# A hybrid attention and state-space block on one core: products without a reader at the start, projection rows without halos, chunk parts in one PSUM bank, another order of units

## The chip, the cores and the metric

The kernel runs on one NeuronCore of a Trainium2 chip. The metric is the device time of one execution in microseconds (us). Three runs of the kernel before took 896.91, 897.30 and 897.51 us; their median is 897.3 us. Five engines work side by side: TensorE (PE, with its weight loads listed as PEld), VectorE (DVE), ScalarE (ACT), GpSimd (POOL) and SyncE (SP, which here only issues DMAs). Every one of them works through its own list of instructions in order; semaphores tie the lists together.

## What is computed

One encoder layer over 16 meta tokens and 512 tokens (528 rows of 1024 features). One normalised input `u` is projected to all columns that two branches need: an attention branch (MLA) and a bidirectional state-space branch (SSD, chunks of 128 rows, 32 heads in 4 groups). Cut to what matters here:

```python
u = rmsnorm(h, norm_w)                       # h = meta tokens and x, 528 rows
proj = u @ w_in                              # 1024 x 8928: q_lat, kv_lat, k_rope, g_attn, z, xbc, dt_raw, merge
xbc = silu(conv(xbc, conv_w, 5 taps) + conv_b)   # along the rows; 3072 columns = x (2048), B (512), C (512)
dt = softplus(dt_raw + dt_bias)
# per direction and chunk c of 128 rows, per head:
y_diag = (C_c B_c^T * decay) @ (x_c * dt_c)
y_off  = exp(cumsum dA) * (C_c @ state_before_c)
y = y_f + y_b + d_skip * x
y = rmsnorm_per_group(y * silu(z)) @ w_ssd_proj
y_a = (softmax(q k^T) v * silu(g_attn)) @ w_attn_proj
out = rmsnorm(h + (sig(gA) * y_a + sig(gS) * y) @ w_out)[16:]
```

## The kernel before

**Numbers.** Large products are made from float32 split into two parts of the type fp32r, a high one and a low one: `hi*hi + lo*hi + hi*lo`. So a projection of 128 output columns over 1024 features is three runs of 8 matmuls. Plain float32 products and transposes are used in the SSD core.

**Layout of u.** `uh` and `ul` (L464, L465) hold the two parts of u transposed, 8 tiles of 128 features by LP = 536 columns: 4 zero columns, 528 rows, 4 zero columns.

**Start.** Four blocks of x rows and the meta rows are loaded (`LOADS`, L478 on). `nwb` is the norm weight, spread over 128 partitions by two one-row products with `ones` (L490 to L492). Per block `u_stats`, `u_scale` and `u_split` (from L571) make the row scale, the scaled rows `xw`, and by 8 transposes into two PSUM banks `tr` the parts `uh` (a cast on ACT) and `ul` (a subtraction on DVE). Blocks go in the order 3, 2, 1, 0, meta.

**Projections.** `proj` (L532) makes a unit of 128 columns. With the tag "d" it writes a PSUM tile of two banks, one half of the 528 rows in each, the second half of the rows first. `conv_tile` (L741) makes 128 columns of x, B or C. Its `proj_halo` computes 270 columns for each half of the rows (`HALO`): 264 and three on each side, so that the convolution needs no column of the other bank. Then ACT multiplies the middle tap, DVE adds the other four taps with `scalar_tensor_tensor`, and a tanh and a last DVE operation make the silu; each of these works on `[128, 2, 264]`. There are 24 such units, 6 for each of the 4 groups (`in_units`). `silu_tile` makes a unit of z or of the attention gate, 512 columns in one bank of the tag "m". There are two tiles of the tag "d" (PSD) and four banks of the tag "m" (PSM).

**SSD core.** Per group g: `ssd_cb`, `ssd_weight` (8 times; makes the weights M of four heads), `ssd_tok` (transposes of x), `ssd_state`, `ssd_cross` (makes `yo`, the part from the state, in two "d" banks) and `ssd_y` (L948). For each of 4 chunks `ssd_y` transposes `yo` into a bank `yt`, adds it to `x4` on DVE, then multiplies x by M into a second bank `yd` (8 float32 products of 64 output columns, two listed matmuls each) and adds that to `x4` too.

**Order.** The kernel records all operations first. `drive` hands out steps of the main chains and of a queue of fill units; `_Recorder.order` then places every operation in a list of its own making, with a table of assumed durations. Nothing is placed by hand but the order in which units enter the queue: the string `"1a2345bcd"` (L1502) for group 0 (digits are conv units of group 0, letters its four z units) and `"zizizizipipipp"` (L1519) for the groups after: `z` a z unit of this group, `i` a conv unit of the next, `p` an output projection unit of the group before. `i` and `p` both wait for the normalisation of the group before (`epi_ok`).

Weights come through two raw buffers `wr` of 512 KB; ACT casts the high part `wh`, DVE makes the low part `wl`.

Of the kernel before, what the change touches and what calls it, by code (L numbers as in the profile page):

```python
# [22 lines left out]
U0 = 4  # L23
LP = U0 + L + 4
HALO = U0 + HALF + 2
# [243 lines left out]
class _Eng:  # L269
# [3 lines left out]
    def __getattr__(self, op):  # L273
        fn = getattr(self.eng, op)

        def call(*args, **kw):
# [31 lines left out]
            if self.name == "PE":  # L308
                if op == "transpose":
# [49 lines left out]
def hybrid_block_kernel(ctx, tc, a, out):  # L359
# [103 lines left out]

    uh = keep([P, KD, LP], F32R, name="uh")  # L464
    ul = keep([P, KD, LP], F32R, name="ul")  # L465
    for t in (uh, ul):
        V.memset(t[:, :, :U0].bitcast(F32), 0.0)
        V.memset(t[:, :, U0 + L:].bitcast(F32), 0.0)
# [6 lines left out]
    for step in LOADS:  # L475
# [7 lines left out]
        else:  # L483
            c = int(step)
            t = xt[c] = big([P, D], name="xt")
            if c == NC:
                Q.dma_start(t[:NM], a["meta_tokens"])
            else:
                S.dma_start(t, a["x"][0, c * P:(c + 1) * P, :])
    nwb = [psm([P, 512], name="nwb") for _ in range(2)]  # L490
    for j in range(2):
        mm(nwb[j], ones[:1, :], nw[j][:1, :])  # L492

# [38 lines left out]
    def proj(w, src, cols, M=P, tag="m", width=HALF):  # L532
# [7 lines left out]
        for h, s in list(enumerate(parts))[::-1]:  # L540
            o = ps[:M, :cols.stop - cols.start] if tag == "m" else ps[:M, h, :width]
# [5 lines left out]
        return o if tag == "m" else ps[:M, :, :width]  # L547

    def proj_all(w, src, M=P):
        return proj(w, src, U_HALVES if src is u_src else HALVES, M, "d")  # L550

    def proj_halo(w):

        return proj(w, u_src, [slice(0, HALO), slice(HALF, HALF + HALO)], P, "d", HALO)

    def halves(ap):
        return ap.rearrange("p (a b) -> p a b", a=2)

    u_src = [(uh[:, k, :], ul[:, k, :]) for k in range(KD)]
    QRY, HALVES = slice(U0 + NM, U0 + L), (slice(0, HALF), slice(HALF, L))  # L560
    U_HALVES = tuple(slice(U0 + s.start, U0 + s.stop) for s in HALVES)

# [24 lines left out]
    def u_split(c):  # L587
        R = rows(c)
        for j in range(2):
# [3 lines left out]
            uc = slice(U0 + col(c).start, U0 + col(c).stop)  # L593
# [56 lines left out]
    def dt_stage():  # L650
# [7 lines left out]
        A.activation(halves(y[:64]), ps[:64], AF.Identity, bias=dtb[:, 0:1])  # L658
        A.copy(halves(kr[64:96]), ps[64:96])
# [81 lines left out]
    def conv_tile(c0, t, out):  # L741
        w = yield from w_cols(c0)
        o = out()
        ps = yield from proj_halo(w)
        wdone()
        yield has("chv")
        at = lambda d: ps[:, :, U0 + d:U0 + d + HALF]
        A.activation(halves(o), at(0), AF.Identity, bias=cb_(t), scale=cw(2, t))
        yield
        for tap in (0, 1, 3, 4):  # L750
            V.scalar_tensor_tensor(halves(o), at(tap - 2), cw(tap, t), halves(o), op0=ALU.mult, op1=ALU.add)
            if tap == 1:
                yield
        yield
        th = ps[:, :, :HALF]
        A.activation(th, halves(o), AF.Tanh, scale=0.5)
        yield
        V.scalar_tensor_tensor(halves(o), th, 1.0, halves(o), op0=ALU.add, op1=ALU.mult)
# [189 lines left out]
    def ssd_y(g):  # L948
        s = grp[g]
        x4 = s["x"]  # L950
        for c in range(NC):
            yield has(("yo", g, c))
            pyo = yield from bank("m", [P, 4, P], "yt")
            for ti in range(4):
                T.transpose(pyo[:, ti, :], s["yo"][c][:, 2 * ti:2 * ti + 2, :].rearrange("p h d -> p (h d)"), ident)
            yield has(("x", g))
            tt(V, x4[:, :, col(c)], x4[:, :, col(c)], pyo, ALU.add)
            drop("m")
            yield has(("M", g, 2 * c), ("t", g, c))
            pyd = yield from bank("m", [P, 4, P], "yd")  # L960
            for hb_ in range(2):
# [3 lines left out]
                for ti in (2 * hb_, 2 * hb_ + 1):  # L965
                    for e in range(2):
                        hh = 2 * ti + e
                        mm(pyd[64 * e:64 * e + 64, ti, :], s["t"][c][:, hh, :], m[:, hh - 4 * hb_, :])
                done.add(("ydh", g, 2 * c + hb_))
            yield  # L970
# [92 lines left out]
    def kvl_unit(t):  # L1063
# [5 lines left out]
        A.copy(halves(z), ps)  # L1069
# [78 lines left out]
    def k_unit(p):  # L1148
# [6 lines left out]
        for e in range(2):  # L1155
            yield lambda: score_ok(2 * p - 2 + e)
            r = slice(64 * e, 64 * e + 64)
            A.copy(halves(kst[r, 2 * e, :]), ps[r])
            yield
            lo_of(V, halves(kst[r, 2 * e + 1, :]), ps[r], halves(kst[r, 2 * e, :]))  # L1160
# [341 lines left out]
    for k in "1a2345bcd":  # L1502
        fill([first[int(k)] if k.isdigit() else zs["abcd".index(k)]], lambda: True)
    for g in range(NG):
# [14 lines left out]
        for k in "zizizizipipipp":  # L1519
# [79 lines left out]
```

## Time and profile before

| what | us |
|---|---|
| three runs, median | 897.3 |
| the profiled execution, its own time | 898.46 |
| its span, first to last instruction | 896.7 |
| PE busy (98% of the span) | 875.1 |
| DVE busy (79%) | 707.8 |
| ACT busy (61%) | 544.2 |

The profile is of one execution. Between its own time and its span lie 1.8 us, which no instruction of the program fills. An engine counts as busy while one of its instructions is under way. Matmuls overlap in the array: a listed matmul of 128x264 lasts some 0.28 us, while the next one starts 0.12 us after it, so the cost of one in a run is the distance between starts. In a timeline row, `x8` says that eight equal instructions follow each other, and the two numbers ahead are the start of the first and the time from there to the end of the last.

### The profile page before, as it was taken

The numbers are of one execution on the slowest core, as the hardware profiler recorded it, in microseconds if no ns is written. First come the engines' busy times: TensorE is split into PE (matmuls) and PEld (weight loads), VectorE is DVE, ScalarE is ACT, GpSimd is POOL, SyncE is SP. The second block draws the span as 40 slices with busy tenths as digits, with TensorE's granted clock in tenths as the row PEclk, the third lists the DMA queues.
The fourth block names the chain that finished last, engine by engine and source line by source line (L and its number), as shares of the span: only waits on it lengthen the run. The fifth ranks groups of instructions, "written<-read, shape, count | busy, mean of one in ns | idle before, by whom it ended". The sixth has DMA issues, their size and how long they took to land.

```text
span 896.7 us, 13288 instructions
## 1 busy us (share of the span) xinstructions
PE 875.1 (98%) x4984; PEld 723.3 (81%) x4984; DVE 707.8 (79%) x1245; ACT 544.2 (61%) x1159; POOL 13.3 (1%) x20
## 2 busy tenths in 40 slices
PE   7999999999999999999999999999999999999996
PEld 5998779877898778866798888888888888778885
DVE  6798699968996699978859757887788978955464
ACT  6359468955794458866235446777577768643232
POOL 1000000000000000000001000000000000000000
PEclk9999999999999999999999999999999999999999
DMA  7255146432533235542223433132213112154322
GB/s 223 72 144 145 51 122 166 110 95 71 163 121 94 61 105 143 141 116 71 71 88 79 114 79 81 32 75 74 59 45 89 36 45 66 48 199 137 99 83 94
DMA packets 129257, 87.50 MB, mean 98 GB/s; under 512 B 26611, under 2 KB 114328, under 8 KB 129194
## 3 DMA queue, kind: packets, MB, share of 16 engines
q1 hardware_dynamic: 129013, 86.53, 34.6%
q8 instruction: 39, 0.64, 0.3%
q14 instruction: 25, 0.20, 0.1%
q10 hardware_dynamic: 180, 0.14, 0.1%
HBM read 82.32 MB, written 4.33 MB: 97 GB/s over the span
## 4 chain that ended last, share of the span: by engine, by line
PE 84%; DVE 9%; ACT 3%; issue 1%; DMA 1%; POOL 0%; POOLq 0%; SPq 0%; ACTq 0%; DVEq 0%
PE pj L266 58%; PE sc L266 4%; PE wo L266 4%; PE pt L266 3%; PE o L266 3%; PE yo L266 2%; PE st L266 2%; PE yd L266 2%; PE tr L266 2%; PE v L266 2%; DVE wl L266 2%; DVE B L266 1%; DMA ar<-cum_rows 1%; DVE C L266 1%; PE yt L266 1%
## 5 line engine op out<-in xcount | busy, mean ns | idle before, releaser
L266 PE MATMUL pj<-uh,wh 128*128 128x270 f32 (+3 forms) x776 | 161.2, 345 | 5.8 <-DVE x L266 3.1
L266 DVE TENSOR_TENSOR wl<-wr,wh 128x1024 fp32r<-128x1024 f32 (+1 forms) x102 | 123.9, 1217 | 54.0 <-ACT wh L266 53.4
L266 PE MATMUL pj<-uh,wl 128*128 128x270 f32 (+3 forms) x776 | 158.9, 338 | 0.0
L266 PE MATMUL pj<-ul,wh 128*128 128x270 f32 (+3 forms) x776 | 151.5, 336 | 0.0
L266 ACT CAST wh<-wr 128x1024 fp32r<-128x1024 f32 (+1 forms) x102 | 106.2, 1041 | 74.6 <-PE pj L266 54.4
L266 PEld LDWEIGHTS pj<-uh,wh 128*128 128x128 f32 (+1 forms) x776 | 120.9, 190 | 26.3 <-issue 6.3
L266 PEld LDWEIGHTS pj<-ul,wh 128*128 128x128 f32 (+1 forms) x776 | 122.6, 188 | 16.2 <-issue 1.3
L266 PEld LDWEIGHTS pj<-uh,wl 128*128 128x128 f32 (+1 forms) x776 | 120.6, 189 | 12.6 <-issue 0.3
L266 ACT ACTIVATE ar<-ar,nacs 128x128 f32<-128x128 f32 x256 | 81.6, 390 | 16.7 <-DMA ar<-cum_rows 16.6
L266 PE MATMUL sc<-kst,qst 96*128 96x264 f32 (+1 forms) x384 | 64.6, 296 | 1.0 <-DVE kst L266 0.3
L266 ACT ACTIVATE p<-sc,mx 128x528 f32<-128x528 f32 x64 | 45.0, 703 | 32.4 <-DVE mx L266 31.3
L266 PEld LDWEIGHTS sc<-kst,qst 96*128 96x128 f32 (+1 forms) x384 | 52.8, 189 | 5.0 <-ACT p L266 2.0
L266 PE MATMUL pt<-cst,p 128*128 128x128 f32 (+1 forms) x320 | 51.2, 273 | 0.4 <-DVE p L266 0.2
L266 DVE SCALAR_TENSOR_TENSOR x<-pj,chv,x 128x528 f32<-128x528 f32 x64 | 48.7, 763 | 0.3
L266 PEld LDWEIGHTS pt<-cst,p 128*128 128x128 f32 (+1 forms) x320 | 37.2, 130 | 12.4 <-DVE p L266 1.1
L266 DVE TENSOR_TENSOR pT<-pt,pT 128x512 fp32r<-128x512 f32 x64 | 43.6, 684 | 3.8 <-ACT pT L266 3.5
L266 DVE TENSOR_REDUCE mx<-sc 128x1 f32<-128x528 f32 x64 | 44.6, 696 | 1.9 <-PE sc L266 1.6
L266 PE MATMUL o<-pT,v 128*128 128x512 f32 x128 | 45.3, 407 | 0.5 <-DVE pT L266 0.5
L266 ACT CAST pT<-pt 128x512 fp32r<-128x512 f32 x64 | 36.7, 588 | 8.9 <-PE pt L266 8.6
L266 ACT ACTIVATE w<-cbm,dt_t 128x128 f32<-128x128 f32 x128 | 40.0, 390 | 0.0
L266 DVE SCALAR_TENSOR_TENSOR w<-cbm,dt_t,w 128x128 f32<-128x128 f32 x128 | 38.7, 346 | 0.3 <-ACT w L266 0.3
L266 PE MATMUL pj<-nh,wh 128*128 128x512 f32 x128 | 38.2, 417 | 0.0
(224 smaller groups left out, 1471.2 us busy)
## 6 DMA issues: line engine op xcount, KB each, us to landing
wr<-in_w_in SPq DMA_DIRECT2D x69, 512.0 KB, 3.9
ar<-cum_rows SPq DMA_DIRECT2D x32, 512.0 KB, 5.6
wr<-in_w_ssd_proj SPq DMA_DIRECT2D x16, 512.0 KB, 3.4
wr<-in_w_attn_proj SPq DMA_DIRECT2D x8, 512.0 KB, 3.6
wr<-in_w_out SPq DMA_DIRECT2D x8, 512.0 KB, 3.5
ws<-in_w_uq SPq DMA_DIRECT2D x36, 64.0 KB, 3.4
xt<-in_x SPq DMA_DIRECT2D x4, 512.0 KB, 5.5
gate_rows<-ma SPq DMA_DIRECT2D x8, 256.0 KB, 2.0
```

The source lines that it names most:

```text
L266: o.fn(*o.args, **o.kw)
```

## The change

- `LP`, `U0` and the zero columns go: `uh` and `ul` hold 528 columns, and their four memsets on DVE are gone.
- In `proj` both halves of a "d" tile are 264 wide. The first half is written to columns 248 to 511 of the first bank, the second to columns 0 to 263 of the second, so the 528 rows lie side by side. `proj_halo` is gone; the convolution reads shifted ranges of the 528 columns and leaves out the one or two columns at the ends.
- `ssd_y` takes one bank per chunk: the transposes of `yo` start the bank's accumulation (as matmuls with the transpose flag), the products with M add to it, and one DVE addition puts the sum into `x4`. The transposes now wait for the first four heads' M as well; the DVE operation waits for x.
- 16 float32 products of 128 columns are written to a tile `idle` of the tag "d" that nobody reads: 6 before the `nwb` products, 2 behind them, 2 for each of the four half blocks of 3 and 2.
- The strings become `"1ab2345cd"` and `"zizizizpipipip"`.

```diff
+    idle = psd([P, 2, 512], name="idle")
+    def keep_busy(lhs, rhs, n):
+        for _ in range(n):
+            mm(idle[:, 0, :rhs.shape[1]], lhs, rhs)
+    keep_busy(ones, ones, 6)
     nwb = [psm([P, 512], name="nwb") for _ in range(2)]
     for j in range(2):
         mm(nwb[j], ones[:1, :], nw[j][:1, :])
+    keep_busy(ident, ones, 2)
...
-            o = ps[:M, :cols.stop - cols.start] if tag == "m" else ps[:M, h, :width]
+            o = ps[:M, :cols.stop - cols.start] if tag == "m" else ps[:M, h, (1 - h) * (512 - HALF):(1 - h) * 512 + h * HALF]
...
                 T.transpose(ps[:, k, :R], xw[c][j][:R, k * P:(k + 1) * P], ident[:R, :R])
+            if c in (3, 2):
+                keep_busy(xw[c][j][:, :P], ones, 2)
...
-        ps = yield from proj_halo(w)
+        ps = yield from proj_all(w, u_src)
...
         for tap in (0, 1, 3, 4):
-            V.scalar_tensor_tensor(halves(o), at(tap - 2), cw(tap, t), halves(o), op0=ALU.mult, op1=ALU.add)
+            d = tap - 2
+            a, b = max(0, -d), L - max(0, d)
+            V.scalar_tensor_tensor(o[:, a:b], ps[:, a + d:b + d], cw(tap, t), o[:, a:b], op0=ALU.mult, op1=ALU.add)
...
-            yield has(("yo", g, c))
-            pyo = yield from bank("m", [P, 4, P], "yt")
+            yield has(("yo", g, c), ("M", g, 2 * c), ("t", g, c))
+            pyd = yield from bank("m", [P, 4, P], "yd")
             for ti in range(4):
-                T.transpose(pyo[:, ti, :], s["yo"][c][:, 2 * ti:2 * ti + 2, :].rearrange("p h d -> p (h d)"), ident)
-            yield has(("x", g))
-            tt(V, x4[:, :, col(c)], x4[:, :, col(c)], pyo, ALU.add)
-            drop("m")
-            yield has(("M", g, 2 * c), ("t", g, c))
-            pyd = yield from bank("m", [P, 4, P], "yd")
+                T.matmul(pyd[:, ti, :], lhsT=s["yo"][c][:, 2 * ti:2 * ti + 2, :].rearrange("p h d -> p (h d)"), rhs=ident,
+                         is_transpose=True, start=(ti == 0), stop=False)
...
-                        mm(pyd[64 * e:64 * e + 64, ti, :], s["t"][c][:, hh, :], m[:, hh - 4 * hb_, :])
+                        mm(pyd[64 * e:64 * e + 64, ti, :], s["t"][c][:, hh, :], m[:, hh - 4 * hb_, :], start=False, stop=(hb_ == 1 and ti == 3))
...
-    for k in "1a2345bcd":
+    for k in "1ab2345cd":
...
-        for k in "zizizizipipipp":
+        for k in "zizizizpipipip":
```

Of the four memsets and the rewritten ranges of `kvl_unit`, `k_unit` and `dt_stage` the diff shows nothing here: they drop the two-part view and are otherwise the same operations.

How the lists of PE stand at three places. **At the start**, before (`nwb`: the norm weight; `tr`: transposes of x rows; `pj`: a projection):

```order
L266 MATMUL nwb_102<-nw_96,ones 128x512
L266 MATMUL nwb_103<-nw_97,ones 128x512
L266 MATMUL tr_133<-cst,xw_111 128x128 x4
L266 MATMUL tr_134<-cst,xw_112 128x128 x4
L266 MATMUL tr_135<-cst,xw_109 128x128 x4
L266 MATMUL tr_136<-cst,xw_110 128x128 x4
L266 MATMUL tr_137<-cst,xw_107 128x128 x4
L266 MATMUL tr_138<-cst,xw_108 128x128 x4
```

and now (`idle`: the products without a reader):

```order
L263 MATMUL idle_102<-ones 128x128 x6
L263 MATMUL nwb_103<-nw_96,ones 128x512
L263 MATMUL nwb_104<-nw_97,ones 128x512
L263 MATMUL idle_102<-ones,cst 128x128 x2
L263 MATMUL idle_102<-ones,xw_112 128x128 x2
L263 MATMUL tr_134<-cst,xw_112 128x128 x4
L263 MATMUL tr_135<-cst,xw_113 128x128 x4
L263 MATMUL idle_102<-ones,xw_113 128x128 x2
L263 MATMUL idle_102<-ones,xw_110 128x128 x2
L263 MATMUL idle_102<-ones,xw_111 128x128 x2
L263 MATMUL tr_136<-cst,xw_110 128x128 x4
L263 MATMUL tr_137<-cst,xw_111 128x128 x4
```

The 16 products stand in front of, between and behind the first transposes; two stand ahead of the first `tr` row and six between the first two blocks and the second.

**In group 0's projections**, from the end of the C unit on, before (512 columns: a z unit; 270: a conv unit; `cr`, `cc`, `ct`: sums over dt, `cb`: the product of C and B):

```order
L266 MATMUL pj_173<-uh,wh_168 128x512 x8
L266 MATMUL pj_173<-uh,wl_169 128x512 x8
L266 MATMUL pj_173<-ul,wh_168 128x512 x8
L266 MATMUL pj_186<-uh,wh_178 128x270 x8
L266 MATMUL pj_186<-uh,wl_179 128x270 x8
L266 MATMUL pj_186<-ul,wh_178 128x270 x8
L266 MATMUL pj_186<-uh,wh_178 128x270 x8
L266 MATMUL pj_186<-uh,wl_179 128x270 x5
L266 MATMUL cr_174<-cst,dat_170 32x128 x4
L266 MATMUL cr_180<-cst,dat_170 32x128 x4
L266 MATMUL cc_187<-dat_170,cst 128x4x32 x2
L266 MATMUL ct_188<-dat_170,ones 128x256
```

and now:

```order
L263 MATMUL pj_174<-uh,wh_168 128x512 x8
L263 MATMUL pj_174<-uh,wl_169 128x512 x8
L263 MATMUL pj_174<-ul,wh_168 128x512 x8
L263 MATMUL pj_186<-uh,wh_179 128x512 x8
L263 MATMUL pj_186<-uh,wl_180 128x512 x8
L263 MATMUL pj_186<-ul,wh_179 128x512 x6
L263 MATMUL cr_176<-cst,dat_173 32x128 x4
L263 MATMUL cr_184<-cst,dat_173 32x128 x4
L263 MATMUL cb_188<-C_171,B_161 128x128 x4
L263 MATMUL pj_186<-ul,wh_179 128x512 x2
L263 MATMUL tr_189<-cst,B_161 128x128 x4
L263 MATMUL pj_195<-uh,wh_182 128x264 x8
```

A second z unit (`pj_186`, 512 columns) now stands ahead of conv unit 2, the 270 became 264, and the product `cb` moved ahead of `cc`.

**In the SSD core of group 0**, the end of the third chunk and the last one, before (`yt`: transposes of `yo`; `yd`: products of x and M; one row `64x128 x4` is half a chunk):

```order
L266 MATMUL pj_317<-ul,wh_273 128x270 x6
L266 MATMUL yd_308<-w_203_307,xtk_241 64x128 x4
L266 MATMUL pj_317<-ul,wh_273 128x270 x2
L266 MATMUL yt_321<-cst,yo_315 128x128 x4
L266 MATMUL pj_324<-uh,wh_294 128x270 x8
L266 MATMUL pj_324<-uh,wl_295 128x270 x8
L266 MATMUL pj_324<-ul,wh_294 128x270 x8
L266 MATMUL pj_324<-uh,wh_294 128x270 x8
L266 MATMUL pj_324<-uh,wl_295 128x270 x8
L266 MATMUL pj_324<-ul,wh_294 128x270 x7
L266 MATMUL yd_325<-w_215_319,xtk_223 64x128 x4
L266 MATMUL yd_325<-w_219_323,xtk_223 64x128 x4
```

and the last chunk now:

```order
L263 MATMUL pj_334<-ul,wh_327 128x512 x6
L263 MATMUL yo_332<-h_313,C_171 128x512
L263 MATMUL pj_334<-ul,wh_327 128x512 x2
L263 MATMUL pj_340<-uh,wh_329 128x512 x3
L263 MATMUL yd_335<-cst,yo_333 128x128 x4
L263 MATMUL pj_340<-uh,wh_329 128x512 x5
L263 MATMUL yd_335<-w_217_321,xtk_238 64x128 x4
L263 MATMUL yd_335<-w_220_324,xtk_238 64x128 x4
L263 MATMUL pj_340<-uh,wl_330 128x512 x8
L263 MATMUL pj_340<-ul,wh_329 128x512 x8
```

The transposes go into `yd` itself and stand close ahead of its products, where a conv unit lay between them before; over the whole list the separate runs of `yd` products go from 28 to 17.

## Rows read from the trace of the kernel before

**Rows 1.** The page: busy time (part 1), granted clock in 40 slices (part 2).

```profile
PE 875.1 (98%) x4984; PEld 723.3 (81%) x4984; DVE 707.8 (79%) x1245; ACT 544.2 (61%) x1159; POOL 13.3 (1%) x20
...
PEclk9999999999999999999999999999999999999999
```

**Rows 2.** Waits of PE, 20 to 430 us: waiter, releaser, total us, times, longest.

```profile
PE pj L266 <- DVE x L266: 3.1, 3, 1.6
PE pj L266 <- DVE yo L266: 2.6, 3, 2.0
```

**Rows 3.** Timeline, PE, first 26 us: start, us, what, count, idle before.

```profile
3.32 3.75 PE L266 MATMUL nwb<-nw,ones 1*128 1x512 f32 x4 [3.32 <-DMA nw<-in_norm_w]
7.32 1.97 PE L266 MATMUL tr<-cst,xw 128*128 128x128 f32 x8 [0.25 <-DVE ss L266]
10.78 1.97 PE L266 MATMUL tr<-cst,xw 128*128 128x128 f32 x8 [1.48 <-DVE ul L266]
13.76 1.97 PE L266 MATMUL tr<-cst,xw 128*128 128x128 f32 x8 [1.01 <-DVE ul L266]
15.55 1.99 PE L266 MATMUL pj<-uh,wh 128*96 128x264 f32 x7
17.33 1.06 PE L266 MATMUL tr<-cst,xw 128*128 128x128 f32 x4
18.04 1.23 PE L266 MATMUL pj<-uh,wh 128*96 128x264 f32 x4
19.07 0.78 PE L266 MATMUL pj<-uh,wl 128*96 128x264 f32 x3
19.68 0.60 PE L266 MATMUL tr<-cst,xw 128*128 128x128 f32 x4
```

**Rows 4.** Timeline, ACT, the same stretch: casts of the second and third block.

```profile
12.42 1.03 ACT L266 CAST uh<-tr 128x512 fp32r<-128x512 f32 x2
...
14.91 0.59 ACT L266 CAST uh<-tr 128x512 fp32r<-128x512 f32 x1 [0.72 <-PE tr L266]
```

**Rows 5.** Timeline, PE, 124 to 138 us: a conv unit, and a run of `yd`.

```profile
128.23 0.66 PE L266 MATMUL yd<-w,xtk 128*64 128x128 f32 x8
128.82 1.13 PE L266 MATMUL st<-xw,bt 128*128 128x512 f32 x2
...
130.79 1.18 PE L266 MATMUL pj<-uh,wl 128*128 128x270 f32 x8
...
135.85 0.60 PE L266 MATMUL yt<-cst,yo 128*128 128x128 f32 x4
136.28 0.71 PE L266 MATMUL tr<-cst,B 128*128 128x128 f32 x5
```

**Rows 6.** Timeline, PE, 446 to 470 us: a kvl unit, and a longer run of `yd`.

```profile
453.83 1.09 PE L266 MATMUL yd<-w,xtk 128*64 128x128 f32 x16
454.86 0.89 PE L266 MATMUL pj<-uh,wl 128*128 128x264 f32 x5
...
459.44 1.14 PE L266 MATMUL pj<-uh,wh 128*128 128x264 f32 x8
...
465.26 0.39 PE L266 MATMUL pj<-uh,wh 128*128 128x512 f32 x1
```

**Rows 7.** Timeline, PE, 530 to 545 us: a unit of 512 columns.

```profile
538.49 2.02 PE L266 MATMUL pj<-uh,wh 128*128 128x512 f32 x8
540.35 2.02 PE L266 MATMUL pj<-uh,wl 128*128 128x512 f32 x8
```

**Rows 8.** Windows, sum of five from 60 to 430 us: busy us by engine.

```profile
sum 370.00, PE 364.33 PEld 295.26 DVE 321.53 ACT 257.23 POOL 3.09; mean PE 72.87 PEld 59.05 DVE 64.31 ACT 51.45 POOL 0.62
```

**Rows 9.** Tile yt: its DVE additions, ns min/median/max, first and last start.

```profile
L266 DVE TENSOR_TENSOR x<-x,yt x16: 678/682/689, 114.0 to 450.0; 128x512 f32<-128x512 f32 x16
```

**Rows 10.** Timeline, 112 to 120 us: DVE and PE around the longest wait.

```profile
114.00 0.68 DVE L266 TENSOR_TENSOR x<-x,yt 128x512 f32<-128x512 f32 x1
...
119.02 1.15 PE L266 MATMUL pj<-uh,wh 128*128 128x270 f32 x7 [1.98 <-DVE yo L266]
```

More of the change, by code (lines that the diff above doesn't have):

```diff
@@ L22 @@
 HALF = L // 2
-U0 = 4
-LP = U0 + L + 4
-HALO = U0 + HALF + 2
 KD = D // P
@@ L308, in call @@
             if self.name == "PE":
-                if op == "transpose":
+                if op == "transpose" or kw.get("is_transpose"):
                     occ, lat = 109.0, 271.0
@@ L462, in hybrid_block_kernel @@
     V.memset(mhalf, -0.5)
[L464 to L468, printed above, removed]
+    uh = keep([P, KD, L], F32R, name="uh")
+    ul = keep([P, KD, L], F32R, name="ul")
     ysacc = keep([P, KD, NX], name="ysacc")
@@ L530, in hybrid_block_kernel, with proj @@
     mid = [False]
-    def proj(w, src, cols, M=P, tag="m", width=HALF):
+    def proj(w, src, cols, M=P, tag="m"):
         hi, lo = w
@@ L546, in proj @@
                     yield
-        return o if tag == "m" else ps[:M, :, :width]
+        return o if tag == "m" else ps.rearrange("p a b -> p (a b)")[:M, 512 - HALF:512 + HALF]
     def proj_all(w, src, M=P):
[L550 to L557, printed above, removed]
+        return proj(w, src, HALVES, M, "d")
     u_src = [(uh[:, k, :], ul[:, k, :]) for k in range(KD)]
-    QRY, HALVES = slice(U0 + NM, U0 + L), (slice(0, HALF), slice(HALF, L))
-    U_HALVES = tuple(slice(U0 + s.start, U0 + s.stop) for s in HALVES)
+    QRY, HALVES = slice(NM, L), (slice(0, HALF), slice(HALF, L))
     def col(c):
@@ L592, in u_split @@
                 T.transpose(ps[:, k, :R], xw[c][j][:R, k * P:(k + 1) * P], ident[:R, :R])
-            uc = slice(U0 + col(c).start, U0 + col(c).stop)
+            if c in (3, 2):
+                keep_busy(xw[c][j][:, :P], ones, 2)
+            uc = col(c)
             A.copy(uh[:, 4 * j:4 * j + 4, uc], ps[:, :, :R])
@@ L657, in dt_stage @@
         yield has("chv")
-        A.activation(halves(y[:64]), ps[:64], AF.Identity, bias=dtb[:, 0:1])
-        A.copy(halves(kr[64:96]), ps[64:96])
+        A.activation(y[:64], ps[:64], AF.Identity, bias=dtb[:, 0:1])
+        A.copy(kr[64:96], ps[64:96])
         drop("d")
@@ L743, in conv_tile @@
         o = out()
-        ps = yield from proj_halo(w)
+        ps = yield from proj_all(w, u_src)
         wdone()
         yield has("chv")
-        at = lambda d: ps[:, :, U0 + d:U0 + d + HALF]
-        A.activation(halves(o), at(0), AF.Identity, bias=cb_(t), scale=cw(2, t))
+        A.activation(o, ps, AF.Identity, bias=cb_(t), scale=cw(2, t))
         yield
         for tap in (0, 1, 3, 4):
-            V.scalar_tensor_tensor(halves(o), at(tap - 2), cw(tap, t), halves(o), op0=ALU.mult, op1=ALU.add)
+            d = tap - 2
+            a, b = max(0, -d), L - max(0, d)
+            V.scalar_tensor_tensor(o[:, a:b], ps[:, a + d:b + d], cw(tap, t), o[:, a:b], op0=ALU.mult, op1=ALU.add)
             if tap == 1:
@@ L754, in conv_tile @@
         yield
-        th = ps[:, :, :HALF]
-        A.activation(th, halves(o), AF.Tanh, scale=0.5)
+        A.activation(ps, o, AF.Tanh, scale=0.5)
         yield
-        V.scalar_tensor_tensor(halves(o), th, 1.0, halves(o), op0=ALU.add, op1=ALU.mult)
+        V.scalar_tensor_tensor(o, ps, 1.0, o, op0=ALU.add, op1=ALU.mult)
         drop("d")
@@ L967, in ssd_y @@
                         hh = 2 * ti + e
-                        mm(pyd[64 * e:64 * e + 64, ti, :], s["t"][c][:, hh, :], m[:, hh - 4 * hb_, :])
+                        mm(pyd[64 * e:64 * e + 64, ti, :], s["t"][c][:, hh, :], m[:, hh - 4 * hb_, :], start=False, stop=(hb_ == 1 and ti == 3))
                 done.add(("ydh", g, 2 * c + hb_))
-            yield
+            yield has(("x", g))
             tt(V, x4[:, :, col(c)], x4[:, :, col(c)], pyd, ALU.add)
@@ L1068, in kvl_unit @@
         yield
-        A.copy(halves(z), ps)
+        A.copy(z, ps)
         drop("d")
@@ L1157, in k_unit @@
             r = slice(64 * e, 64 * e + 64)
-            A.copy(halves(kst[r, 2 * e, :]), ps[r])
+            A.copy(kst[r, 2 * e, :], ps[r])
             yield
-            lo_of(V, halves(kst[r, 2 * e + 1, :]), ps[r], halves(kst[r, 2 * e, :]))
+            lo_of(V, kst[r, 2 * e + 1, :], ps[r], kst[r, 2 * e, :])
             done.add(("k", 2 * p + e))
```

## The prediction

> **What bounds the kernel now.** I read the page first. TensorE is busy 98% of the span, DVE 79%, ACT 61% [rows 1]. So what takes time off PE's own list counts fully, and what takes work off another engine counts only where PE waits for it. Next, the waits of PE. From 20 to 430 us, which holds the whole state-space part, it waits 5.7 us in six places, always for a DVE operation that frees a PSUM tile [rows 2]. The start is the other weak place: up to 13.76 us PE stands idle for 3.32 + 0.25 + 1.48 + 1.01 = 6.1 us [rows 3]. The busy share hides a second loss there. Eight transposes of 128 columns take from 13.76 us to the next row at 15.55 us, 0.22 us each [rows 3]; later four take from 135.85 to 136.28 us, 0.11 us each [rows 5]: at the start PE runs at 1.2 GHz of its 2.4. The clock line of the page shows its full level from the first slice [rows 1], so at the start the distance between matmuls is the reading, not that line. The pace doubles between the rows at 19.07 and 19.68 us, after projections had run without a pause from 15.55 us; the transposes and the `nwb` products ahead had not brought it [rows 3].
>
> **Part 1: 264 columns for 270.** 24 conv units of 48 matmuls are 1152 matmuls, each six columns shorter, all on PE. Forty of 270 columns take 135.85 - 130.79 = 5.06 us, 126.5 ns each [rows 5]; 48 of 264 take 465.26 - 459.44 = 5.82 us, 121.3 ns each [rows 6]. The difference is 5.2 ns, times 1152 is 6.0 us. The other bound is the slope to 512 columns: eight in 540.35 - 538.49 = 1.86 us are 232.5 ns [rows 7], so 111 ns for 248 columns, 2.7 ns for six, 3.1 us in all. I take 4.7 us. It is nearer to the first, because the 264 rows are the same operation on the same tiles, and below it because some of the units of group 0 run where DVE sets the pace. The Trainium skill (TensorE: Matmul & The Clock Gate, section Back-to-back issue gap) gives a distance of N/2.4 + 2.5 ns at full clock: an estimate from it is 2.5 ns for six columns, 2.9 us in all. The rows lie above its distance by 9 ns at 264 columns. By that rule the sum below would be 1.8 us smaller.
>
> The convolution's ACT and DVE operations read 528 columns in a row across two banks in place of two times 264. No row shows such a read. The element count is the same and the first and last taps lose one or two columns; I take 0, with 0.05 us either way for each of its six operations. They lie beside PE work, so it matters only where PE waits for DVE.
>
> **Part 2: one bank and one addition per chunk.** PE keeps the same 64 transposes and 128 products. DVE loses 16 additions of 0.68 us, 10.9 us [rows 9]. On PE the number of separate runs of `yd` falls from 28 to 17 in the list. A run of half a chunk (8 listed matmuls) takes 128.82 - 128.23 = 0.59 us [rows 5], one of a whole chunk (16) 454.86 - 453.83 = 1.03 us [rows 6]; so a run costs 2 x 0.59 - 1.03 = 0.15 us beside its work, and 11 fewer give 1.7 us. I take 1.6 us, bounds 0 and 2.5 us, since the row before such a run may lengthen too.
>
> The new wait: the transposes of `yo` stand behind the first half's M. Queued behind them on PE is whatever the list puts there, and the recorder puts them where it thinks M is ready. The bank `yd` is not held longer than before, since it was already held over the wait for the second M.
>
> **Part 3: fewer waits for DVE.** DVE is busy 321.5 of the 370 us from 60 to 430 us [rows 8]; 10.9 us less is 3% of that time. At the longest wait the removed work is directly in line: an addition of `yt` runs from 114.00 us ahead of the `yo` operations that PE waits for until 119.02 us [rows 10], and without it that wait of 1.98 us shrinks by 0.68. The first string puts a z unit ahead of conv unit 2: PE work that gives DVE time for its backlog of dt steps and taps. Of the 5.7 us [rows 2] I take 2.5 us as gained. The list is placed anew, though, and the waits come where its assumed durations are wrong; the bounds are 5.5 us gained and, as many again, 5.7 us lost.
>
> **Part 4: the start.** The 16 products are pairs of passes of 128 columns. At the half clock a pass costs about what a transpose does, 0.21 to 0.22 us [rows 3], so a product 0.43 us and all of them 6.9 us; at the full clock half. Six run while PE waits for the first norm weight until 3.32 us, and nearly fit. Two stand ahead of the first transposes (0.86 us): these end later, but ACT is late there too. Six stand between the first and the second block, in the pause of 1.48 us [rows 3]: at half clock they need 2.6 us and overrun it by 1.1 us, at full clock 1.3 us and fit.
>
> What they can give is the clock. If it is up before 13.76 us, the third block's transposes are done 0.8 us sooner, of which ACT, which sat 0.72 us for them before the cast at 14.91 us [rows 4], takes at most 0.7 us. From 15.55 to 19.68 us PE does 14 products and 4 transposes in 4.13 us [rows 3]; at the later distances (121 ns [rows 6] and 108 ns [rows 5]) they need 2.14 us. So the most is 0.7 + 2.0 = 2.7 us. If the clock rises no sooner, the second block's transposes begin near 12.7 us in place of 10.78 us; its casts on ACT ran at 12.42 us [rows 4] and would run near 13.8 us: a loss of 1.4 us. I take 2.0 us gained, because the casts and subtractions of the last blocks hold PE back once it is fast. Where this cover fails, the loss bound holds. The Trainium skill (TensorE: Matmul & The Clock Gate, section What's actually happening) says that "the default state is throttled, and activity releases the throttle", which the pace at 19.68 us bears out; it adds that the point does not start with the kernel and so varies from run to run, which one trace cannot show.
>
> The `idle` tile takes one of the two "d" tiles, but is free before the second projection needs it. The dropped memsets and the changed `kvl`, `k` and dt views cost and give nothing: DVE waits for the first rows anyway.
>
> **Sum.** 4.7 + 1.6 + 2.5 + 2.0 = 10.8 us. The profiled execution, 898.46 us with a span of 896.7 us, would come to 887.7 us and 885.9 us. It lies 1.2 us over the median of 897.3 us; I take the sum off the median: **886.5 us**.
>
> **The rivals.**
> (a) *The products don't bring the clock up sooner*, and the change doesn't do there what it says. For it: transposes and one-row products from 3.32 to 15.73 us did not [rows 3], and the new products fill less than half of that time. Against it: the projections from 15.55 us did. The start then loses 1.4 us: 886.5 + 3.4 = 889.9 us.
> (b) *The waits form again elsewhere.* PE's list is all new in the state-space part, and DVE is still busy (321.5 - 10.9) / 370, 84% of it [rows 8, 9]. With nothing gained from part 3, 889.0 us; with as many waits again, 894.7 us.
> (c) *Columns cost by the slope*, and the 5.2 ns are a peculiarity of two stretches: 3.1 in place of 4.7 us, 888.1 us. The formula from the Trainium skill (TensorE: Matmul & The Clock Gate, Back-to-back issue gap) would make it 888.3 us.
> (d) *Slower: the later conv units lay the core bare.* In the first string group 0's last four conv units come one unit later, in the second the last one of groups 2 and 3 (group 1's string holds conv units alone); so three cores start one unit later, while as much other work as before has been used up ahead of them. A unit of 24 matmuls of 512 columns is 24 x 232.5 ns = 5.6 us [rows 7]. If PE finds nothing in its place, three times 5.6 are 16.7 us: 886.5 + 16.7 = 903.2 us. It decides for slower from 12.6 us on, 4.2 us per group. Against it: PE waits 5.7 us in all for these 410 us [rows 2], the list still has conv or projection units between the steps of each core, and the string moves work and removes none.
>
> **How the numbers follow.** The forecast, all four parts with their sign, 0.55; (a) 0.13; (b) 0.18; (c) 0.09; (d) 0.05. The range takes the forecast's own spread, some 4 us down (6.0 us for the columns, 2.7 at the start, 4.0 for the waits), and reaches up over (a), (c) and most of (b): 882 to 892.5 us. A measurement of this kernel can tell about 0.2%, 1.8 us, from no change. Faster by more than that: the forecast, (a), (c) and nearly all of (b), 0.92; within it, the upper end of (b) with (a), 0.03; slower, (d), 0.05.
>
> **What would show it.** In the new profile: 48 matmuls of a conv unit in 5.8 us, not 6.0; transposes of the second and third block 0.11 us apart and the first projection near 15 us, with the row that answers to 24 us some 2 us earlier; DVE busy near 697 us (707.8 less 10.9); 17 runs of `yd`; and waits of PE from 20 to 430 us near 3 us. It is wrong if the half pace lasts to 19 us, or if those waits pass 10 us.

## The result, and the profile after

The changed kernel takes 888.0 us (median of four runs, 887.58 to 888.39) where the kernel before took 897.25 us (four runs, 896.91 to 897.51): a ratio of 0.9891, interval 0.9876 to 0.9906, or 9.25 us less. The forecast was 886.5 us. The profiled execution took 887.58 us with a span of 885.7 us, 11.0 us less than the profiled one of before.

The page, busy time and clock, answers to [rows 1]; the waits of PE from 20 to 430 us answer to [rows 2]:

```profile
PE 867.5 (98%) x5016; PEld 720.4 (81%) x5016; DVE 699.2 (79%) x1225; ACT 544.1 (61%) x1159; POOL 13.9 (2%) x20
...
PEclk9999999999999999999999999999999999999999
```

```profile
PE pj L263 <- DVE yo L263: 1.7, 2, 1.1
PE pj L263 <- DVE x L263: 1.7, 2, 0.8
PE pj L263 <- ACT h L263: 1.2, 1, 1.2
```

PE is busy 7.6 us less though it has 32 listed matmuls more, DVE 8.6 us less. The waits are 4.6 us where they were 5.7 us, and none is longer than 1.2 us; so the waits alone are not where the gain is.

The start, timeline of PE, answers to [rows 3]:

```profile
1.05 2.93 PE L263 MATMUL idle<-ones 128*128 128x128 f32 x12 [1.05 <-DVE ones L263]
3.91 2.25 PE L263 MATMUL nwb<-nw,ones 1*128 1x512 f32 x4
7.25 0.71 PE L263 MATMUL idle<-ones,cst 128*128 128x128 f32 x4 [1.08 <-DMA cst<-in_masks]
7.79 0.95 PE L263 MATMUL idle<-ones,xw 128*128 128x128 f32 x4
8.54 1.91 PE L263 MATMUL tr<-cst,xw 128*128 128x128 f32 x8
10.24 2.02 PE L263 MATMUL idle<-ones,xw 128*128 128x128 f32 x12
12.10 1.04 PE L263 MATMUL tr<-cst,xw 128*128 128x128 f32 x8
14.60 1.25 PE L263 MATMUL tr<-cst,xw 128*128 128x128 f32 x8 [1.46 <-DVE ul L263]
15.93 0.72 PE L263 MATMUL pj<-uh,wh 128*96 128x264 f32 x4
...
23.62 1.13 PE L263 MATMUL pj<-uh,wh 128*96 128x264 f32 x8
```

The transposes of the first block still go at half pace (8 in 1.91 us), those of the second at full pace (8 in 1.04 us). Windows of the same stretch show where the granted clock rises for good (behind the window: its length, PE's busy time and count, the clock, the DMA share and GB/s):

```profile
8.00:11.30 3.30, 3.30 (x17) 0.50 1.16 229
11.40:15.00 3.60, 2.15 (x20) 1.00 0.53 130
```

In the records of the granted clock the lasting rise is at 11.32 us; it was at 19.61 us before. (The page's clock line shows full speed wherever there is no record yet, so the distance between rows is the reading for a start.) But the first and third blocks begin later than before, 8.54 for 7.32 us and 14.60 for 13.76 us, and the first projection stands at 15.93 us, not near 15. The row at 23.62 us stood at 24.59 us before: 1.0 us gained in this execution.

A conv unit and the first chunk of group 0's `yd`, timeline of PE, answer to [rows 5] and [rows 6]:

```profile
117.38 1.14 PE L263 MATMUL pj<-uh,wl 128*128 128x264 f32 x8
...
122.23 0.60 PE L263 MATMUL yd<-cst,yo 128*128 128x128 f32 x4
122.76 1.09 PE L263 MATMUL yd<-w,xtk 128*64 128x128 f32 x16
123.79 1.12 PE L263 MATMUL st<-xw,bt 128*128 128x512 f32 x2
```

Forty matmuls of 264 columns in 4.85 us are 121.3 ns each. The transposes of `yo` and both halves of the chunk's products stand together, in 1.56 us.

### The profile page after: what moved, and what is told of

Same layout as the page of the kernel before. It is cut to its first block, busy times and chain, and to the rows that moved or that the text cites. A ratio compares the mean times of both kernels' runs of the same rounds, so it can differ in the third digit from the quotient of the medians.

```text
span 885.7 us, 13331 instructions
## 1 busy us (share of the span) xinstructions
PE 867.5 (98%) x5016; PEld 720.4 (81%) x5016; DVE 699.2 (79%) x1225; ACT 544.1 (61%) x1159; POOL 13.9 (2%) x20
## 4 chain that ended last, share of the span: by engine, by line
PE 81%; DVE 11%; ACT 4%; issue 1%; DMA 1%; POOL 0%; POOLq 0%; ACTq 0%; DVEq 0%
PE pj L263 57%; PE wo L263 4%; PE sc L263 4%; PE pt L263 3%; PE yd L263 3%; PE o L263 3%; PE yo L263 2%; PE st L263 2%; DVE wl L263 2%; DVE x L263 2%; PE v L263 1%; PE tr L263 1%; DVE w L263 1%; DVE h L263 1%; DVE pT L263 1%
## 5 line engine op out<-in xcount | busy, mean ns | idle before, releaser
L263 PE MATMUL pj<-uh,wh 128*128 128x264 f32 (+2 forms) x776 | 159.1, 342 | 5.1 <-DVE yo L263 1.7
L263 PE MATMUL pj<-uh,wl 128*128 128x264 f32 (+2 forms) x776 | 155.8, 335 | 0.0
L263 PE MATMUL pj<-ul,wh 128*128 128x264 f32 (+2 forms) x776 | 150.6, 335 | 0.0
L263 PEld LDWEIGHTS pj<-uh,wh 128*128 128x128 f32 (+1 forms) x776 | 118.9, 188 | 25.1 <-issue 5.4
L263 PEld LDWEIGHTS pj<-uh,wl 128*128 128x128 f32 (+1 forms) x776 | 118.7, 188 | 13.2 <-issue 0.7
L263 DVE SCALAR_TENSOR_TENSOR x<-pj,chv,x 128x526 f32<-128x526 f32 (+1 forms) x64 | 48.7, 761 | 1.7 <-ACT x L263 1.4
```

The costliest lines, as they stand in the source:

```text
L263: o.fn(*o.args, **o.kw)
```

## The experiments

All times below are medians; a ratio is to the kernel before in runs of the same chip, taken over all runs, so it is not the quotient of the two medians. The experiments ran in three groups, each with its own runs of before (medians 897.86, 897.22 and 898.16 us), so a difference to the 888.0 us of the changed kernel is taken to be good to about 1.5 us. "Waits" are PE's from 20 to 520 us; "core spans" are, from the timelines, the time from the first to the last product of `yd` of a group, summed over the four groups. With two banks the first half of a chunk's products may stand ahead of the transposes of `yo` (in group 0 of before at 106.4 and 113.1 us), with one bank it can't; so part of a difference in core spans is where the count starts.

| run | strings | banks per chunk | columns | us | ratio, interval | waits | core spans | last `yd` |
|---|---|---|---|---|---|---|---|---|
| before | old | 2 | 270 | 897.3 | 1 | 5.7 | 191 | 454.7 |
| e1_columns | old | 2 | 264 | 897.05 | 0.9980 (0.9967–0.9994) | 6.9 | 189 | 450.7 |
| e2_onebank | old | 1 | 270 | 898.57 | 1.0003 (0.9993–1.0013) | 9.6 | 152 | 453.1 |
| e4_order | new | 2 | 270 | 911.97 | 1.0152 (1.0131–1.0173) | 15.7 | 216 | 484.5 |
| e9_strings_one_bank | new | 1 | 270 | 896.01 | 0.9972 (0.9958–0.9986) | 6.0 | 169 | 456.0 |
| e7_old_strings* | old | 1 | 264 | 896.7 | 0.9991 (0.9980–1.0001) | 10.1 | 155 | 449.0 |
| e8_two_banks* | new | 2 | 264 | 903.39 | 1.0064 (1.0048–1.0081) | 13.0 | 203 | 475.4 |
| changed kernel* | new | 1 | 264 | 888.0 | 0.9891 (0.9876–0.9906) | 4.6 | 156 | 449.6 |
| e6_columns_back* | new | 1 | 270 | 890.56 | 0.9918 (0.9902–0.9934) | 3.4 | 157 | 453.1 |

Those with * have the 16 products; runs e3, e5 and e12, below, are on these alone, and e10 and e11 on one string each.

**The columns, alone and taken back.** e1_columns puts the layout without halos into the kernel before. The planner goes on assuming the duration of 270 columns, so that PE's list is the same one:

```diff
-        ps = yield from proj_halo(w)
+        ps = yield from proj_all(w, u_src, P, "pjc")
...
+            if any(x.name.startswith("pjc") for x in aps):
+                n = {264: 270, 526: 528, 527: 528}.get(n, n)
```

> The kernel before with the 264-column layout alone (rows across two banks, no halos); the recorder still counts 270, so the lists of PE, ACT and SP stay as they were. Theory, columns at 126 against 121.5 ns as read in the two profiles: 1152 x 4.5 ns = 5.2 us, less what is lost where DVE sets the pace: 4.5 to 5.2 us faster, a ratio of 0.994 to 0.995. Rival, slope of 2.7 ns for six columns: 3.1 us, 0.9965. Rival, that the gain goes back into the waits for DVE: under 2 us, above 0.998.

897.05 us, ratio 0.9980: some 1.8 us (0.5 to 3.0 by the interval; the medians lie 0.8 us apart), far below the theory's 4.5 us. Matched row by row from 27 us on, the conv rows (1136 of them) are 4.0 us shorter in sum and all others 1.6 us longer; 2.4 us are left. The waits of PE, 20 to 430 us, of this run:

```profile
PE pjc L263 <- DVE yo L263: 2.7, 3, 2.1
PE pjc L263 <- DVE x L263: 1.8, 2, 1.3
PE pj L263 <- DVE x L263: 1.6, 1, 1.6
PE rb L263 <- DVE rc L263: 0.6, 1, 0.6
PE cr L263 <- DVE dat L263: 0.2, 1, 0.2
```

They are 6.9 us where before had 5.7 us: PE is sooner at the places where DVE is not ready. e6_columns_back does the reverse in the changed kernel, with the lists of PE, DVE and ACT unchanged:

```diff
-            o = ps[:M, :cols.stop - cols.start] if tag == "m" else ps[:M, h, (1 - h) * (512 - HALF):(1 - h) * 512 + h * HALF]
+            o = ps[:M, :cols.stop - cols.start] if tag == "m" else ps[:M, h, (1 - h) * (512 - HALF - wide):(1 - h) * 512 + h * (HALF + wide)]
+            s = slice(s.start - wide, s.stop) if wide and h == 0 else slice(s.start, s.stop + wide) if wide else s
...
-        ps = yield from proj_all(w, u_src)
+        ps = yield from proj(w, u_wide, W_HALVES, P, "d", 6)
```

> The changed kernel with 270 columns again in the 24 conv units (six of them over zero columns or rows of the other half that nobody reads, written ahead of or behind the 264 that are read); the lists of PE, DVE and ACT are the same, instruction for instruction, and POOL clears the added columns at the start. Theory (PE bounds, 1152 matmuls 5 ns longer each, fully on the path): 888.0 + 5.5 = 893.5 us. Rival 1 (as with the columns alone on the old kernel, half of it is given back in waits): 890.5 us. Rival 2 (slope to 512 columns): 891.1 us, with a distance of 124 ns between starts in place of 126.

890.56 us: 2.6 us more than the changed kernel, nearest to rival 1, with rival 2 at 891.1 us not told from it by time but by the distance. The same conv unit in this run's timeline of PE:

```profile
119.63 1.19 PE L263 MATMUL pj<-uh,wl 128*128 128x270 f32 x8
...
124.68 0.60 PE L263 MATMUL yd<-cst,yo 128*128 128x128 f32 x4
```

Forty in 5.05 us, 126.3 ns: the distance differs by 5.0 ns, as the rows of before said, and not by 2.7. Matched row by row from 27 us on, 1131 conv rows are 4.6 us longer, and the rows around them 2.7 us shorter (1.2 us of that are waits); 1.9 us are left. So the distance is right, and about half of it is time.

**The products, alone, taken out, and with other operands.** e3_products adds the 16 products and nothing else to the kernel before; e5_no_products takes them from the changed kernel, whose lists are otherwise the same but for two projection matmuls that change places on PE ahead of 24 us:

```diff
-    keep_busy(ones, ones, 6)
...
-    keep_busy(ident, ones, 2)
...
-            if c in (3, 2):
-                keep_busy(xw[c][j][:, :P], ones, 2)
```

> The kernel before with the 16 products alone; from the second projection on PE's list is that of before. Theory, from the profile after (the clock rises at 4.5 us, falls at 7.9 and rises for good at 11.3): the row that stood at 24.59 us comes 1.0 us sooner, and 0.8 to 1.0 us stay to the end, 0.999. Rival, the start's gain is lost in the waits at 61 and 70 us, where DVE sets the pace: under 0.3 us. Rival, the forecast's 2.0 us: 0.9978.

> The changed kernel without its 16 products and the tile idle; all four engines' lists are otherwise the same, instruction for instruction. Theory (the products bring the clock up sooner, and that is worth what the row at 24 us of before moved, 1.0 us): 888.0 + 1.0 = 889.0 us, half pace of the matmuls until 16 to 20 us, the waits behind 24 us unchanged. Rival 1 (products worth the predicted 2.0 us): 890.0 us. Rival 2 (products are worth nothing, as alone on the old kernel): 888.0 us or less.

e3_products took 898.32 us, ratio 1.0007 (0.9996 to 1.0019); e5_no_products 888.1 us, ratio 0.9891 (0.9874 to 0.9907). In time the products are worth nothing that can be told. The start of PE in e5_no_products:

```profile
2.15 4.09 PE L263 MATMUL nwb<-nw,ones 1*128 1x512 f32 x4 [2.15 <-DMA nw<-in_norm_w]
7.26 1.97 PE L263 MATMUL tr<-cst,xw 128*128 128x128 f32 x8 [1.02 <-DVE ss L263]
10.63 1.97 PE L263 MATMUL tr<-cst,xw 128*128 128x128 f32 x8 [1.40 <-DVE ul L263]
13.61 1.97 PE L263 MATMUL tr<-cst,xw 128*128 128x128 f32 x8 [1.01 <-DVE ul L263]
15.40 1.97 PE L263 MATMUL pj<-uh,wh 128*96 128x264 f32 x7
...
24.63 1.13 PE L263 MATMUL pj<-uh,wh 128*96 128x264 f32 x8
```

Here the norm weight is there at 2.15 us, and the six products in front make PE come to it at 3.91 us. All three blocks of transposes begin 1.0 to 1.5 us sooner than with the products, but the half pace lasts to 19.7 us, and the row that counts is 1.0 us later. From there on the two executions differ by 0.35 us the other way. Over all profiles the row lies at 23.62, 24.70, 22.98, 23.70, 24.26, 23.16 and 24.67 us with the 16 products (the changed kernel, e6, e7, e8, e10, e11, e3), and at 24.59, 23.06, 24.37, 24.52, 24.63 and 24.70 us without products (before, e1, e2, e4, e5, e9): 0.4 us apart in the mean, with 1.6 to 1.7 us between the ends of either set. e12_other_products gives the products behind the `nwb` products and those of the blocks other operands, and puts six in place of the two behind `nwb`, to fill the pause of 1.08 us ahead of 7.25 us. So it has 20 products and not 16, and its expectation is wrong in saying that all else is the same:

```diff
-    keep_busy(ident, ones, 2)
+    keep_busy(xt[2][:, :P], ones, 6)
...
-                keep_busy(xw[c][j][:, :P], ones, 2)
+                keep_busy(xw[c][j][:, :P], ident, 2)
```

> The changed kernel with other operands for ten of its 16 products: six behind the norm weight's products work on the rows of block 2 as loaded, so that they need no masks and fill the pause of 1.1 us ahead of the first transposes, and the products of a block take its rows and the unit matrix. All else in the lists is the same. Theory (the products gave little because the clock fell back to half from 7.91 to 11.32 us): full pace through the first transposes, the row that answers to 24 us 0.5 to 1.0 us sooner, 887.0 to 887.5 us. Rival (the start is bound by ACT and DVE and by the loads, so a held clock gives nothing): row at 23.6 us as in the changed kernel, 888.0 us.

It took 889.3 us (ratio 0.9905, 0.9891 to 0.9920), and neither theory fits: the row is late. The start of PE:

```profile
3.91 3.78 PE L263 MATMUL nwb<-nw,ones 1*128 1x512 f32 x4
7.62 2.93 PE L263 MATMUL idle<-ones,xt 128*128 128x128 f32 x12
10.34 1.06 PE L263 MATMUL idle<-cst,xw 128*128 128x128 f32 x4
11.20 1.91 PE L263 MATMUL tr<-cst,xw 128*128 128x128 f32 x8
...
26.29 1.13 PE L263 MATMUL pj<-uh,wh 128*96 128x264 f32 x8
```

This time the clock had not risen by the `nwb` products (3.78 us where they took 2.25), although the same six products stood ahead of them, so the six in the pause took 2.93 us and pushed the first transposes to 11.20 us. The lasting rise came at 13.51 us, with PE 2.7 us behind; at 0.23 us a pass (7.62 to 10.34 us for 12) the four added products are an estimated 1.8 us of that. Whether a clock held throughout would pay stays open.

**One bank per chunk, alone and taken back.** e2_onebank puts the new `ssd_y` into the kernel before, e8_two_banks the old one into the changed kernel:

```diff
-                T.matmul(pyd[:, ti, :], lhsT=s["yo"][c][:, 2 * ti:2 * ti + 2, :].rearrange("p h d -> p (h d)"), rhs=ident,
-                         is_transpose=True, start=(ti == 0), stop=False)
+                T.transpose(pyo[:, ti, :], s["yo"][c][:, 2 * ti:2 * ti + 2, :].rearrange("p h d -> p (h d)"), ident)
+            yield has(("x", g))
+            tt(V, x4[:, :, col(c)], x4[:, :, col(c)], pyo, ALU.add)
```

> The kernel before with the one bank and one addition per chunk alone. Theory, fewer runs of yd and 10.9 us less on DVE: runs 1.5 us, waits of PE from 20 to 430 us down from 5.7 to some 4 us: 2.5 to 3.5 us faster, 0.996 to 0.997. Rival, the DVE work lay beside PE and the list alone decides: within 1 us, 0.999 to 1.001, with as many waits. Rival, the transposes wait for M and PE behind them: slower, 1.001 or more, with a wait of PE for DVE w or for yd.

> The changed kernel with two banks per chunk again: transposes of yo into a bank of their own, a second DVE addition of 0.68 us per chunk. Theory (with the new strings the SSD core of group 3 ends too late, and what rescues it is the one bank, 16 DVE operations fewer): PE runs out of other work behind 470 us, a wait of 5 us or more for the sums of squares there and the clock at half for some 20 us: 900 us or more. Rival (the shorter conv units rescue it, not the one bank): no such wait, 889 to 891 us.

Alone, nothing: 898.57 us, ratio 1.0003. Taken back, 15.4 us lost: 903.39 us. The core spans are shorter with one bank, 152 us in place of 191 us, 2.4 us per chunk, where an addition itself takes 0.68 us [rows 9]. Counted from the first transposes of `yo` they are 154.5 us in place of 180.9 us: 11.0 and 12.0 us less in groups 0 and 2, 3.3 and 0.1 us less in groups 1 and 3. The 26.4 us are work of other units in PE's list, not waits for DVE: all waits of PE in that stretch are 5.7 us before. In the kernel before, every one of the 16 additions of `yt` starts within 0.8 us of the end of its transposes, and the products don't read what it writes. The last chunk of group 0 in the kernel before, PE and below it DVE:

```profile
151.80 0.60 PE L266 MATMUL yt<-cst,yo 128*128 128x128 f32 x4
...
158.22 1.09 PE L266 MATMUL yd<-w,xtk 128*64 128x128 f32 x16
```

```profile
149.57 0.69 DVE L266 TENSOR_TENSOR w<-w,ar 128x512 f32<-128x512 f32 x1
...
152.77 0.68 DVE L266 TENSOR_TENSOR x<-x,yt 128x512 f32<-128x512 f32 x1
```

The weights M of the chunk are done at 150.26 us and the addition at 153.45 us, but the products stand at 158.22 us, behind 47 matmuls of a conv unit and without a wait. The code says where that can come from: with two banks the addition ended a step of `ssd_y`, and between two steps `drive` may hand out work of other units; with one bank the transposes and the first half's products are one step. No run separates the addition from the step that it ended. In the old order the shorter cores buy no time; the waits of PE even grow, to 9.6 us. With the new order they decide: with two banks the waits from 20 to 430 us fall to 1.7 us (1.4 us in e4_order), but the core of group 3 begins its transposes at 440.2 us instead of 409.9 us, since the cores of groups 1 and 2 end 10.7 and 22.5 us later. The last part of group 3's core in e8_two_banks, timeline of PE (`ssq`, `rb`: the normalisation; `nh`: the high part of normalised rows):

```profile
474.98 0.66 PE L263 MATMUL yd<-w,xtk 128*64 128x128 f32 x8 [1.64 <-DVE w L263]
...
482.18 1.78 PE L263 MATMUL ssq<-ones,sq 128*128 128x1 f32 x8 [4.47 <-DVE sq L263]
486.79 1.12 PE L263 MATMUL rb<-cst,rc 128*128 128x128 f32 x4 [2.83 <-DVE rc L263]
489.39 4.71 PE L263 MATMUL pj<-nh,wh 128*128 128x512 f32 x13 [1.49 <-ACT nh L263]
```

The last product of `yd` comes at 475.4 us instead of 449.6. DVE is busy 24.96 of the 25 us from 455 to 480 us; PE waits 10.4 us in these four rows, with nothing else in between that is ready, and the granted clock falls to half from 482.3 to 492.5 us: the 13 matmuls of 512 columns from 489.39 us on take until 493.94 us, 350 ns each in the mean, where they take 232 ns elsewhere [rows 7]. So the theory of e8_two_banks holds in time and place; it had named 20 us at half and a wait of 5 us, where 10.2 and 4.5 us came.

**The strings, alone and taken back, both and one by one.**

```diff
-    for k in "1ab2345cd":
+    for k in "1a2345bcd":
...
-        for k in "zizizizpipipip":
+        for k in "zizizizipipipp":
```

> The kernel before with the two new strings alone. Theory, the order moves work and removes only waits: the waits of PE from 20 to 430 us go from 5.7 to 3 to 5 us, 1 to 3 us faster, 0.997 to 0.999. Rival, later conv units lay the cores bare: up to 5.6 us slower for each of three cores, ratio above 1.002, with waits of PE at the ends of groups. Rival, nothing: 0.9995 to 1.0005.

> The changed kernel with the two old strings of unit order. Theory (the strings are what turns the other parts into time, since the three others alone give 0.8, 0 and 0 us): about 896 us, with waits of PE of 6 us and more between 20 and 430 us. Rival 1 (the strings are harmful in themselves, as alone on the old kernel, where they cost 14 us, and the other parts bear them): faster than 888.0 us. Rival 2 (the strings make no difference once the chunk parts lie in one bank): 887 to 889 us.

> The changed kernel with group 0's old string alone (conv unit 2 ahead of the second z unit); the string of the later groups stays new. Theory (the old first string brings the wait of 3 us for B ahead of 45 us and the half pace behind it, 1.4 us): 888.0 + 4.4 = 892.4 us. Rival (all of the 8.7 us that both old strings cost lies in the order of the later groups): 888 us.

> The changed kernel with the old string of the later groups alone (two output projection units at the end, conv units earlier); group 0's string stays new. Theory (the rest of the 8.7 us): 888.0 + 4.3 = 892.3 us, with more waits of PE for DVE from 90 to 360 us than the 2.5 us + 1.2 us of the changed kernel, none before 90 us beyond 0.8 us. Rival (all lies in the first string): 888 us.

The new strings alone make the kernel before slower, 911.97 us: group 3's core ends at 484.5 us and PE is bare behind it. The longest wait and the clock of that stretch, from e4_order's waits and windows (busy time and count of PE, PEld, DVE, ACT and POOL, then the clock, 0.52):

```profile
PE ssq L266 <- DVE sq L266: 7.6, 1, 7.6
```

```profile
480.00:505.00 25.00, 12.73 (x50) 9.47 (x51) 21.03 (x39) 9.35 (x17) 1.01 (x1) 0.52 0.30 77
```

In the changed kernel the same strings are what gains: with both old ones it takes 896.7 us, as the theory said, with the first old one 895.07 us (ratio 0.9966, 0.9952 to 0.9979), with the second old one 889.44 us (0.9911, 0.9896 to 0.9927). So the first string is worth 7 us there and the second 1 to 2 us, near what these runs can tell; the theories of e10 and e11, 4.4 and 4.3 us, shared it out wrongly. The place in e10_old_first_string, PE and below it DVE:

```profile
41.13 2.01 PE L263 MATMUL pj<-ul,wh 128*128 128x512 f32 x8
46.12 1.21 PE L263 MATMUL pj<-uh,wh 128*128 128x264 f32 x8 [2.98 <-DVE B L263]
```

```profile
43.20 0.76 DVE L263 SCALAR_TENSOR_TENSOR C<-pj,chv,C 128x526 f32<-128x526 f32 x1
...
44.27 0.68 DVE L263 SCALAR_TENSOR_TENSOR z<-z,pj 128x512 f32<-128x512 f32 x1
44.87 0.49 DVE L263 SCALAR_TENSOR_TENSOR dt_t<-dt_t,dte 128x320 f32<-128x320 f32 x1
45.27 0.70 DVE L263 SCALAR_TENSOR_TENSOR B<-pj,B 128x528 f32<-128x528 f32 x1
```

Conv unit 2 needs one of the two "d" tiles; the units of B and C hold both, and DVE ends B only at 45.97 us, behind the taps of C and the steps of dt. In the changed kernel the second z unit stands there (24 matmuls of 512 columns from 42.35 us on), which goes to the four banks of the tag "m", and the wait is gone. In the profile of e7_old_strings, with the same wait (2.97 us), the clock fell to half from 45.1 to 48.5 us as well; in that of e10 it did not. In e10 the waits sum to 9.3 us, 4.7 more than in the changed kernel; its profile ends 5.9 us later, 0.6 of which it has lost by 24 us.

**Strings and one bank on the kernel before.**

> The kernel before with the two new strings and one bank per chunk; 270 columns and the layout with zero columns stay, no products. Theory (strings and one bank need each other: alone they gave +14 and 0 us, without either the changed kernel loses 9 and 15 us; the columns are worth 2.6 and the products nothing): 897.2 - 9.2 + 2.6 = 890.6 us, no wait for the sums of squares behind 470 us. Rival (the new strings fit only the list that comes with the 264 columns): 900 us or more, with PE out of work behind 470 us as with the strings alone.

896.01 us, between theory and rival; by the ratio, strings and one bank give 2.5 us (1.3 to 3.8) on the list of the kernel before. The core of group 3 is not bare (last `yd` at 456.0 us, waits 6.0 us), so the one bank does rescue the strings. But 5.4 us are missing to e6_columns_back, which has the same parts (and the products), and as it differs another list, from the planner's 264-column durations, and the rows without halos. Of the 5.7 us between the two profiles 2.6 us are waits; another 1.7 us is a fall of the clock from 466.8 to 470.2 us, behind a run of 26 `ssq` matmuls of one column (e6 has them as 16 and 10, and no fall); 1.4 us I could not place.

## Why the prediction came out right, point by point

The total was 1.5 us too low and inside the range. That it came so near is in part luck: by the runs the columns were put 2.1 us too high, the products 1.9 us too high, and parts 2 and 3 together 2.4 us too low. The terms were not independent, as the sum took them to be.

- **Part 1, 4.7 us.** The distance was read rightly (5.0 ns in the runs); that it counts fully "all on PE" was the step that failed. Measured: 2.6 us taken back, 1.8 us alone. The rows around the conv rows give back 1.6 to 2.7 us, part of it in waits that PE reaches sooner. Rival (c) named nearly the right time for the wrong reason; so did the formula of the Trainium skill (TensorE: Matmul & The Clock Gate, section Back-to-back issue gap), with an estimate of 2.5 ns and 2.9 us, where the rows show 5.0 ns. The long reads across two banks cost nothing: the taps take 0.76 us in the rows of DVE above, as in the kernel before.
- **Parts 2 and 3, 1.6 + 2.5 us.** The runs of `yd` are 17, DVE is at 699.2 us (697 said), and the waits from 20 to 430 us are 4.6 us (3 said). What fell is the pricing by parts. One bank alone 0, strings alone +14 us, both with the columns 6.5 us of gain (9.25 less 2.6 for the columns and 0.1 for the products). The wait of 1.98 us that the prediction picked did shrink, to 0.62 us in e2, but others grew. The step that failed is the one that counted runs of `yd` and a share of the waits. What the new strings need are cores that end early enough; as far as the traces show, one bank gives that by bringing a chunk's transposes and products together in PE's list, which is more than the 0.68 us of an addition.
- **Part 4, 2.0 us.** The clock did rise 8 us sooner, against rival (a). The bound from below was the better end: the products delay the first transposes by 1.2 us (four of them stand ahead of these, from 7.25 to 8.54 us, where the prediction counted two), and of the gain of pace 1.0 us is left at the row of 24 us in the profile, 0.4 us in the mean of all, and 0.1 us in the medians.
- **Rival (b).** The waits did not form again in the changed kernel. They did with one bank and the old strings (9.6 and 10.1 us, e2 and e7).
- **Rival (d).** Its mechanism is real and was underrated: later conv units lay the core bare. It turns on how late the core ends, which the prediction didn't look at: with two banks it costs 14 to 15 us (e4, e8), with one bank nothing. Its price of three times 5.6 us was near in size, but it was one place, the end of group 3: of e4's 14 us, 10.0 us are waits (15.7 less 5.7), and behind 480 us the clock is at half.

Taken together: 2.6 us for the columns, about nothing for the products, and 6.5 us that are left for order and bank. On the list planned for 270 columns order and bank give only 2.5 us (e9), so some 4 us of the 6.5 come with what else differs, which points to the list that the planner makes for 264 columns. It is not shown: no run has 264 columns with the new strings and one bank on a list planned for 270. A count by rows would have hidden this. From 27 us on, by the distances between starts without waits, the rows of 264 and 270 columns take 166.5 us in place of 172.5, the float32 rows of the SSD core 82.0 in place of 86.3, and the waits 7.3 in place of 8.2; that looks like the forecast's sum, but what a part is worth only the runs with it taken back tell.

## What to carry to other kernels

Where a program makes its own list, an operation that splits a chain into steps can cost what the planner puts between the steps, not its own duration; look at how late the chain ends, then at whether enough other work is left to cover its end. Price an order and a shortening of the chain together, since either alone can be worth nothing or a loss (0 and 14 us here). Where an edit also changes the planner's list, hold the list to price the edit by itself. A shorter matmul on a bound engine can give part of its gain back: here about half of it was time.

## What the runs showed of the hardware

The same first instructions of PE met two histories of the clock. With the six products in front, the `nwb` products took 2.1 to 2.25 us in four profiles (the changed kernel, e7, e8, e11: a rise to full at 4.2 to 4.5 us, then half again, full for good near 11 us) and 3.78 us in four others (e3, e6, e10, e12: no rise before 10.6 to 13.5 us). The prediction quoted the Trainium skill (TensorE: Matmul & The Clock Gate, section What's actually happening) for a point that varies from run to run; these profiles agree that it does, but by far more than the ±500 ns that the section gives. So a start of this kind has to be judged over several executions, and a product put into a pause costs more where the rise has not come: four passes took 0.54 us in the changed kernel (7.25 to 7.79 us, at full) and 0.86 us in e12 (10.34 to 11.20 us, at half).
